# One decoder layer on one core: the pace at which modulation products are asked for during attention, 0.8 per unit throughout, becomes 1.5 in the first half and 0.6 in the second

## The chip, the core and the metric

The kernel runs on one core of a Trainium2 chip. Its engines work side by side, each in the order of its own instruction list: TensorE (PE; its weight loads are shown as PEld), VectorE (DVE), ScalarE (ACT), GpSimd (POOL) and SyncE (SP), which here does nothing but issue transfers, one after another. The metric is device time in microseconds for one execution, median of several runs; lower is better.

## The reference, cut to what matters

```python
mod = silu(c) @ w_ada + b_ada            # (1, 6 * 2048): six rows of 2048
sh1, sc1, gt1, sh2, sc2, gt2 = split(mod, 6)
h = rms_norm(x, g_pre_mix) * (1 + sc1) + sh1
proj = h @ w_in                          # q, k, v of 3 branches, gates, RG-LRU x and y
o_att = nsa_attention(...)               # 16 heads, 4 key groups, 512 queries
o_rnn = gelu(yr) * rg_lru(conv(xr))
x = x + gt1 * rms_norm(concat(norms of o_att, o_rnn) @ w_out, g_post_mix)
h = rms_norm(x, g_pre_mlp) * (1 + sc2) + sh2
x = x + gt2 * rms_norm(square(relu(h @ w_ff1)) @ w_ff2, g_post_mlp)
```

SEQ is 512, D_MODEL 2048, D_FF 8192, all in float32. The six rows of `mod` need 6 x 2048 dot products of length 2048 with `silu(c)`. Rows 0 and 1 are needed first, row 2 (`gt1`) in the output projection, rows 3 and 4 (`sh2`, `sc2`) at its end, row 5 (`gt2`) at the very end.

## The kernel before

The dot products for rows 2 to 5 are done on VectorE. One **product** (`qdot`, L219) loads a piece of `w_ada` (128 x 512, 256 KB, tile `md`) and multiplies it with a quarter of `silu(c)` that is copied to all partitions (tile `ca`), with the sum over its 512 columns as a by-product. A row has 64 products: 4 quarters by 16 pieces. The tile `ca` has one buffer, so the next quarter is loaded (L217) only when the 16th product of the one before has been done. The tiles `md` form a ring of 4 (`NMD`) during attention and share a ring of 6 (`NTMP`) in the output projection. Both loads are issued by SP, in the same list as the loads of the other weights (`wr`, L85: 512 KB each from `win`, `wv` or `wout`), which have a ring of their own of 2. A tool of the language sets the order of the instructions of each engine: it may put an instruction that is ready ahead of others that the code asks for earlier.

The stages that matter here, in order:

1. The first half of attention, `attention(0, n1)`: 64 units (a head, a branch, 128 queries). A unit takes scores (L727, L728 on TensorE), a softmax (`soft1` L737 and `soft2` L747 to L749 on VectorE and ScalarE), transposes (L756), the split of the transposed probabilities into two parts (`evac_t` L767, L768), and every fourth unit the product with the values (`pv` L783). `cmp_a` to `cmp_b` (L686 to L717) do the compressed branch. In between, TensorE works on the rest of the input projection (`proj`, L178 to L180), whose weights are split into a high and a low part (`sl`, L103 on ScalarE and L104 on VectorE), and the recurrent group runs (L804 to L850).
2. A transition: the keys, queries and values of the second pair of groups (L241, L254, L303).
3. The second half, `attention(1, n3 - n2)`, again 64 units.
4. The output projection: 4 column blocks of 512, 16 steps of k each, 4 x 3 matmuls of 512 columns per step (L916 to L918), results times `gbc` (L1073), with the remaining products of rows 3 and 4 spread over 36 steps (`cdots`), then residual and transposes.
5. The MLP, in which the products of row 5 are done at places of their own.

During attention, each of the 70 steps of a half adds `MRATE` to a counter, and a product is asked for each time it reaches 1. All products of row 2 come first, then row 4, then row 3. What is left of rows 4 and 3 is divided evenly over the steps of the output projection: `nd_ = [0.0, (len(QD[3]) + len(QD[4])) / 36.0]`.

Of the kernel before, what the change touches and what calls it, by code (L numbers as in the profile page):

```python
# [27 lines left out]
Q_REST, K_REST, XR_T, YR_T = 0, 6, 8, 16  # L28


NA1, NA2, NMS, NTMP, NXI, NPC, NSB, TD, MRATE, NMD, NRT = 4, 10, 22, 6, 4, 2, 11, 3, 0.8, 4, 6
JOIN = [2, 1, 1, 1] * 5 + [2, 1, 1, 0, 3]
KQ = 6
HALF, CA_ = 512, 1
# [97 lines left out]
def hybrid_block_kernel(ctx: ExitStack, tc: tile.TileContext, xT, c, vec, wada, wst, win, wv0, wv1,  # L132
# [125 lines left out]
    def fill(n):  # L258
        for _ in range(n):
            if stream:  # L260
                stream.pop(0)()
# [411 lines left out]
    def quad(pair, ep):  # L673
        return [((2 * pair + i % 2), 2 * ep + i // 2) for i in range(4)]
# [3 lines left out]
    def cmp_a(pair, ep):  # L678
        hs = quad(pair, ep)
        p_ = bp.tile([128, 4, 4, 32], F32, name="pc", tag="pc", bufs=1)  # L680
        for c2 in range(2):
            sc = ps("pj").rearrange("p (c e r n) -> p c e r n", c=2, e=4, r=2)
            for c_ in range(2):
                ch = 2 * c2 + c_
                for i, (g, e_) in enumerate(hs):
                    T.matmul(sc[:, c_, i].rearrange("p r n -> p (r n)"), Q[4 * g + e_][:, 128 * ch:128 * ch + 128],  # L686
                             kc[:, g].rearrange("p r n -> p (r n)"), start=True, stop=True)
            pv_ = p_[:, 2 * c2:2 * c2 + 2]
            V.tensor_add(pv_, sc[:, :, :, 0], maskc[:, 2 * c2:2 * c2 + 2, None, :].to_broadcast([128, 2, 4, 32]))
            V.tensor_add(pv_, pv_, sc[:, :, :, 1])  # L690
        m_ = bp.tile([128, 16], F32, name="cmx", bufs=1)
        d_ = bp.tile([128, 16], F32, name="cdn", bufs=1)
        pf = p_.rearrange("p c e n -> p (c e) n")
        V.reduce_max(m_, pf, axis=AX.X)
        V.tensor_sub(pf, pf, m_[:, :, None].to_broadcast([128, 16, 32]))
        A.activation(p_, p_, AF.Exp, scale=0.125)
        PC[pair, ep] = [p_, d_]

    def cmp_a2(pair, ep):
        p_, d_ = PC[pair, ep]  # L700
        pf = p_.rearrange("p c e n -> p (c e) n")
        V.reduce_sum(d_, pf, axis=AX.X)
        V.reciprocal(d_, d_)
        for i, (g, e_) in enumerate(quad(pair, ep)):
            dv = d_.rearrange("p (c e) -> p c e", c=4)[:, :, i]
            V.tensor_mul(dv, dv, gates[:, :, 3 * (4 * g + e_)])
        V.tensor_mul(pf, pf, d_[:, :, None].to_broadcast([128, 16, 32]))

    def cmp_b(pair, ep):
        p_, d_ = PC[pair, ep]  # L710
        pt = ps("pj")
        for ch in range(4):
            T.transpose(pt[:, 128 * ch:128 * ch + 128], p_[:, ch].rearrange("p e n -> p (e n)"), ident)
        ph = bp.tile([128, S], F32R, name="pch", bufs=1)
        pl = bp.tile([128, S], F32R, name="pcl", bufs=1)
        A.activation(ph, pt, AF.Copy)
        V.tensor_sub(pl, pt, f(ph))  # L717
        PC[pair, ep] = (ph, pl)
# [3 lines left out]
    def scores(u):  # L722
        h, br, ch = u
        n = 128 * (ch + 1)
        sp_ = ps("S")
        q_ = Q[h][:, 128 * ch:128 * ch + 128]
        T.matmul(sp_[:, :n], q_, KD[h // 4][:, br, 0, :n], start=True, stop=False)  # L727
        T.matmul(sp_[:, :n], q_, KD[h // 4][:, br, 1, :n], start=False, stop=True)  # L728
        UN[u] = [sp_]

    def soft1(u):
        h, br, ch = u
        n = 128 * (ch + 1)
        sp_ = UN[u][0]
        p_ = bp.tile([128, S], F32, name="pp", tag="pp", bufs=TD + 1)
        sm = bp.tile([128, 4], F32, name="sm", tag="sm", bufs=6)
        V.tensor_tensor_reduce(p_[:, :n], sp_[:, :n], mask[:, S - n:], scale=-0.125, scalar=3e38,  # L737
                               op0=OP.add, op1=OP.min, accum_out=sm[:, 0:1])
        A.activation(p_[:, :n], p_[:, :n], AF.Exp, bias=sm[:, 0:1], scale=-1.0, accum_out=sm[:, 1:2])
        UN[u] = [p_, sm]  # L740

    def soft2(u):
        h, br, ch = u
        n = 128 * (ch + 1)
        p_, sm = UN[u]
        gi = h * 3 + 1 + br
        V.reciprocal(sm[:, 2:3], sm[:, 1:2])  # L747
        V.tensor_mul(sm[:, 3:4], sm[:, 2:3], gates[:, ch, gi:gi + 1])
        A.activation(p_[:, :n], p_[:, :n], AF.Copy, scale=sm[:, 3:4])  # L749

    def trans(u):
        h, br, ch = u
        p_ = UN[u][0]
        pt = ps("T")
        for j in range(ch + 1):
            T.transpose(pt[:, 128 * j:128 * j + 128], p_[:, 128 * j:128 * j + 128], ident)  # L756
        UN[u] = [pt]

    def evac_t(u):
        h, br, ch = u  # L760
        n = 128 * (ch + 1)
        if ch == 0:
            HB[h, br] = [bp.tile([128, 13, 128], F32R, name=n_, bufs=1) for n_ in ("pth", "ptl")]
        th, tl = HB[h, br]
        pv_ = UN.pop(u)[0][:, :n].rearrange("p (j q) -> p j q", q=128)
        sl = slice(ch, 3 * ch + ch + 1, 3)
        A.activation(th[:, sl], pv_, AF.Copy)  # L767
        V.tensor_sub(tl[:, sl], pv_, f(th[:, sl]))  # L768
# [3 lines left out]
    def pv(h, br, i, pc):  # L772
        g = h // 4
        if br == 0:
            OT["o"] = ps("O")
            T.matmul(OT["o"], vcz[:, i], pc[0], start=True, stop=False)
            T.matmul(OT["o"], vcz[:, i], pc[1], start=False, stop=False)
        o = OT["o"]
        for j in range(4):
            v_ = VV[g][:, j, br].rearrange("p r d -> p (r d)")  # L780
            for x_, t_ in enumerate(HB[h, br]):
                m_ = t_[:, 4 * j:3 * j + 4].rearrange("p a b -> p (a b)")
                T.matmul(o[:, 128 * j:], v_, m_, start=False, stop=br == 1 and j == 3 and x_ == 1)  # L783

    def head_out(h, i, t):
        half = i % 2
        if half == 0:
            OT["t"] = bp.tile([128, S], F32, name="ot", bufs=1)
        ot, o = OT["t"], OT["o"]
        ol = rt("ol")  # L790
        A.activation(ol[0:64], o[64:128], AF.Copy)
        V.tensor_add(ot[64 * half:64 * half + 64], o[0:64], ol[0:64])
        if half:
            G.dma_start(oat[t], ot)
            add_sq(0, ot, t == 0)
# [150 lines left out]
    nmod = [0.0]  # L946

    def attention(pair, natoms):
        seq, info = [], {}
        for ep in range(2):  # L950
            for i, (g, e_) in enumerate(quad(pair, ep)):
                for br in range(2):
                    for ch in range(4):
                        u = (4 * g + e_, br, ch)
                        info[u] = (ep, i, 4 * pair + e_)
                        seq.append(u)
        n = len(seq)
        goal, done = len(stream) - natoms, 0
        for s_ in range(-1, n + TD + 2):
            def get(k):  # L960
                return seq[k] if 0 <= k < n else None
            if get(s_ - 1):
                soft2(get(s_ - 1))
            if get(s_ - TD - 1):
                evac_t(get(s_ - TD - 1))
            if get(s_):
                soft1(get(s_))
            if 0 <= s_ < n and s_ % 32 == CA_:
                cmp_a(pair, s_ // 32)
            if get(s_ + 1):  # L970
                scores(get(s_ + 1))
            tot = natoms * (s_ + 2) // (n + TD + 3)
            k = tot - done
            fill(k // 2)
            if get(s_ - TD):
                trans(get(s_ - TD))
            fill(k - k // 2)
            done = tot
            if 0 <= s_ < n:
                if s_ % 32 == CA_ + 1:  # L980
                    cmp_a2(pair, s_ // 32)
                if s_ % 32 == CA_ + 2:
                    cmp_b(pair, s_ // 32)
            u = get(s_ - TD - 1)
            if u and u[2] == 3:
                ep, i, t = info[u]
                pv(u[0], u[1], i, PC[pair, ep])
                if u[1] == 1:
                    head_out(u[0], i, t)
            nmod[0] += MRATE  # L990
            while nmod[0] >= 1:
                qdot(bp, 2 if QD[2] else 4 if QD[4] else 3, 1)
                nmod[0] -= 1
        fill(natoms - done)

    vcz_fill(0)
    attention(0, n1)
    evac_k(OT["k0"], 0, 1)
    evac_k(OT["k1"], 1, 1)
# [766 lines left out]
```

## Time and profile before

| what | value |
|---|---|
| median of 3 runs | 2195.1 us (2194.03 to 2197.76) |
| the profiled execution's own time | 2198.01 us |
| its span, first to last instruction | 2196.3 us |
| mean granted TensorE clock | 0.98 of full speed |
| TensorE, VectorE, ScalarE busy | 95%, 86%, 63% of the span |

The profile comes from one execution; durations are read from it. It began at 2196.3 us of span and took 1.7 us more around it, and was 2.9 us above the median of the runs.

### The profile page before, as it was taken

What the parts mean: (1) busy time and instruction counts of PE and PEld (TensorE: products, weight loads), DVE (VectorE), ACT (ScalarE), POOL (GpSimd) and SP (SyncE); (2) the same over time, 40 slices, a digit from 0 to 9 for tenths busy, and PEclk for the clock granted to TensorE, in tenths of its full rate; (3) what the DMA queues carried; (4) which work ended last, traced back from release to release, by engine and by line L of the source; (5) the groups of instructions that cost most, each with busy time, mean ns of one, the idle gap of its engine ahead of it and who ended that gap; (6) DMA issues with size and microseconds to landing.
All of it is one profiled execution on the core that took longest, in us unless ns stands there. A gap on an engine that the chain in (4) does not pass through costs nothing.

```text
span 2196.3 us, 39416 instructions
## 1 busy us (share of the span) xinstructions
PE 2095.3 (95%) x14621; PEld 1915.0 (87%) x14621; DVE 1878.7 (86%) x3764; ACT 1392.9 (63%) x2536; POOL 65.4 (3%) x121
## 2 busy tenths in 40 slices
PE   7998999999999989899999999998999999999995
PEld 3687777778877867899999999998999999999995
DVE  8987999877887677889999999998998878887788
ACT  4349879548995226765555555555866777767764
POOL 0000000000000000000000000000000000000010
PEclk8999999999999989999999999999999999999998
DMA  9764554662126886555555555566775444444453
GB/s 375 304 240 136 191 159 151 212 208 68 59 79 216 281 295 207 173 190 176 183 184 169 174 176 189 187 229 213 276 234 185 172 157 140 169 147 159 138 170 116
DMA packets 136802, 411.12 MB, mean 187 GB/s; under 512 B 16209, under 2 KB 23265, under 8 KB 132257
## 3 DMA queue, kind: packets, MB, share of 16 engines
q1 hardware_dynamic: 123970, 340.43, 45.9%
q0 software_dynamic: 12640, 68.17, 9.0%
q8 instruction: 115, 1.88, 0.3%
q14 instruction: 77, 0.63, 0.1%
HBM read 366.58 MB, written 41.97 MB: 186 GB/s over the span
## 4 chain that ended last, share of the span: by engine, by line
PE 64%; DVE 16%; DMA 8%; ACT 7%; issue 4%; SPq 0%; DVEq 0%; POOL 0%; ACTq 0%; POOLq 0%
PE ps_pj L1133 3%; DMA md<-wada 3%; PE ps_pj L1134 3%; PE ps_pj L1135 3%; PE ps_pj L1480 3%; PE ps_pj L1481 3%; PE ps_pj L1482 3%; DVE fl L1301 3%; PE ps_T L1135 2%; PE ps_T L1133 2%; PE ps_T L1134 2%; PE ps_S L1133 2%; PE ps_S L1134 2%; PE ps_S L1135 2%; PE ps_S L1480 2%
## 5 line engine op out<-in xcount | busy, mean ns | idle before, releaser
L1300 ACT ACTIVATE fh<-fs 128x1024 fp32r<-128x1024 f32 x256 | 272.9, 1066 | 326.8 <-DVE fs L1319 126.4
L1301 DVE TENSOR_TENSOR fl<-fs,fh 128x1024 fp32r<-128x1024 f32 x256 | 312.4, 1220 | 100.8 <-ACT fh L1300 98.2
L1300 ACT ACTIVATE fh<-fr 128x768 fp32r<-128x768 f32 (+2 forms) x296 | 217.2, 735 | 74.5 <-PE ps_pj L1134 12.9
L1301 DVE TENSOR_TENSOR fl<-fr,fh 128x768 fp32r<-128x768 f32 (+2 forms) x296 | 240.2, 814 | 14.4 <-ACT fh L1300 14.2
L103 ACT ACTIVATE sl<-wr 128x512 fp32r<-128x512 f32 (+2 forms) x252 | 145.5, 606 | 150.0 <-DMA wr<-wout 98.2
L104 DVE TENSOR_TENSOR sl<-wr,sl 128x512 fp32r<-128x512 f32 (+2 forms) x252 | 163.5, 662 | 46.9 <-ACT sl L103 32.2
L1316 DVE TENSOR_TENSOR fs<-fr 128x512 f32<-128x512 f32 x256 | 175.2, 684 | 8.2 <-DMA fr<-wff 6.6
L1480 PE MATMUL ps_pj<-fh,AH 128*128 128x256 f32 x602 | 168.9, 281 | 0.3 <-ACT ps_pj L1460 0.2
L1481 PE MATMUL ps_pj<-fl,AH 128*128 128x256 f32 x602 | 168.8, 281 | 0.0
L1482 PE MATMUL ps_pj<-fh,AL 128*128 128x256 f32 x602 | 168.2, 280 | 0.0
L178 PE MATMUL ps_pj<-AH,sl 128*128 128x512 f32 x384 | 162.4, 423 | 0.1
L219 DVE SCALAR_TENSOR_TENSOR md<-md,ca 128x512 f32<-128x512 f32 x192 | 127.3, 685 | 40.8 <-DMA md<-wada 23.3
L180 PE MATMUL ps_pj<-AH,sl 128*128 128x512 f32 x384 | 153.7, 400 | 2.0 <-DVE sl L104 1.9
L179 PE MATMUL ps_pj<-AL,sl 128*128 128x512 f32 x384 | 153.7, 400 | 0.0
L1480 PEld LDWEIGHTS ps_pj<-fh,AH 128*128 128x128 f32 x602 | 113.9, 189 | 0.9 <-ACT ps_pj L1460 0.9
L1481 PEld LDWEIGHTS ps_pj<-fl,AH 128*128 128x128 f32 x602 | 114.0, 189 | 0.2 <-DVE fl L1301 0.2
L1482 PEld LDWEIGHTS ps_pj<-fh,AL 128*128 128x128 f32 x602 | 113.6, 189 | 0.0
L1481 PE MATMUL ps_S<-fl,AH 128*128 128x256 f32 x394 | 110.8, 281 | 2.6 <-DVE fl L1301 2.6
L1480 PE MATMUL ps_S<-fh,AH 128*128 128x256 f32 x394 | 110.8, 281 | 2.0 <-ACT fh L1300 1.6
L1481 PE MATMUL ps_T<-fl,AH 128*128 128x256 f32 x396 | 110.9, 280 | 0.2 <-DVE fl L1301 0.2
L1480 PE MATMUL ps_T<-fh,AH 128*128 128x256 f32 x396 | 110.9, 280 | 0.0
L1482 PE MATMUL ps_T<-fh,AL 128*128 128x256 f32 x396 | 110.8, 280 | 0.0
(637 smaller groups left out, 7332.4 us busy)
## 6 DMA issues: line engine op xcount, KB each, us to landing
fr<-wff SPq DMA_DIRECT2D x276, 512.0 KB, 3.8
md<-wada SPq DMA_DIRECT2D x256, 256.0 KB, 4.5
uf<-ud POOLq DMA_DIRECT2D x32, 896.0 KB, 4.9
wr<-win SPq DMA_DIRECT2D x48, 512.0 KB, 3.7
ada<-wada SPq DMA_DIRECT2D x22, 1024.0 KB, 10.6
wr<-wout SPq DMA_DIRECT2D x36, 512.0 KB, 4.7
ud<-uf POOLq DMA_DIRECT2D x18, 896.0 KB, 5.3
ud<-uf POOLq DMA_DIRECT2D x14, 768.0 KB, 4.9
```

The source lines that it names most:

```text
L104: self.nc.vector.tensor_sub(lo, raw, self.f(hi))
L178: T.matmul(o, wh, mh, start=start, stop=False)
L179: T.matmul(o, wh, ml, start=False, stop=False)
L1133: T.matmul(o, wh, b[0], start=start, stop=False, skip_group_check=True)
L1134: T.matmul(o, wh, b[1], start=False, stop=False, skip_group_check=True)
L1135: T.matmul(o, wl, b[0], start=False, stop=stop, skip_group_check=True)
L1300: A.activation(hi, src, AF.Copy)
L1301: V.tensor_sub(lo, src, f(hi))
L1316: V.tensor_add(v2(Sm[:, :512]), v2(R[:, 256:768]), R[:, None, :256].to_broadcast([128, 2, 256]))
L1480: T.matmul(o, uh, hi, start=first and k < 4 and t_ == 0, stop=False, skip_group_check=True)
L1481: T.matmul(o, uh, lo, start=False, stop=False, skip_group_check=True)
L1482: T.matmul(o, ul, hi, start=False, stop=last, skip_group_check=True)
```

## The change

The rate becomes a pair, one number for each half of attention.

```diff
-NA1, NA2, NMS, NTMP, NXI, NPC, NSB, TD, MRATE, NMD, NRT = 4, 10, 22, 6, 4, 2, 11, 3, 0.8, 4, 6
+NA1, NA2, NMS, NTMP, NXI, NPC, NSB, TD, MR, NMD, NRT = 4, 10, 22, 6, 4, 2, 11, 3, (1.5, 0.6), 4, 6
...
-            nmod[0] += MRATE
+            nmod[0] += MR[pair]
             while nmod[0] >= 1:
                 qdot(bp, 2 if QD[2] else 4 if QD[4] else 3, 1)
                 nmod[0] -= 1
```

Where the products of rows 2, 3 and 4 then stand in VectorE's list:

| stage | before | of the change |
|---|---|---|
| first half of attention, up to its 64th `soft1` | 72 | 96 |
| transition, up to the 65th `soft1` | 40 | 40 |
| second half of attention | 0 | 10 |
| output projection | 80 | 46 |

VectorE in the first half, from the third to the next first chunk of queries of a branch (39th to 41st unit; `sm` and `pp` are the softmax, `ptl` the low part of the transposed probabilities, `sl` the low part of a split weight). Before:

```order
L737 ISA pp,sm<-ps_S,mask 128x384
L737 ISA sm 128x1
L748 TENSOR_TENSOR sm<-sm,gates 128x1
L737 ISA pp,sm<-ps_S,mask 128x512
L737 ISA sm 128x1
L768 TENSOR_TENSOR ptl<-ps_T,pth 128x3x128
L104 TENSOR_TENSOR sl<-wr,sl 128x512
L747 RECIPROCAL sm<-sm 128x1
L737 ISA pp,sm<-ps_S,mask 128x128
```

Of the change, the same units:

```order
L737 ISA pp,sm<-ps_S,mask 128x384
L737 ISA sm 128x1
L219 SCALAR_TENSOR_TENSOR md,dq_91<-md,ca 128x512 x2
L747 RECIPROCAL sm<-sm 128x1
L768 TENSOR_TENSOR ptl<-ps_T,pth 128x4x128
L748 TENSOR_TENSOR sm<-sm,gates 128x1
L737 ISA pp,sm<-ps_S,mask 128x512
L737 ISA sm 128x1
L104 TENSOR_TENSOR sl<-wr,sl 128x512
L219 SCALAR_TENSOR_TENSOR md,dq_91<-md,ca 128x512
L737 ISA pp,sm<-ps_S,mask 128x128
```

Where there were none, three products stand now between two softmaxes and the next; the splits and softmaxes keep their places.

VectorE at the end of the transition, from the last queries (`qd`, L254) to the second `soft1` of the second half. Before:

```order
L254 TENSOR_TENSOR qd<-ps_pj,qd 64x512 x2
L104 TENSOR_TENSOR sl<-wr,sl 128x512 x2
L737 ISA pp,sm<-ps_S,mask 128x128
L737 ISA sm 128x1
L747 RECIPROCAL sm<-sm 128x1
L748 TENSOR_TENSOR sm<-sm,gates 128x1
L737 ISA pp,sm<-ps_S,mask 128x256
```

Of the change:

```order
L254 TENSOR_TENSOR qd<-ps_pj,qd 64x512
L219 SCALAR_TENSOR_TENSOR md,dq_92<-md,ca 128x512
L254 TENSOR_TENSOR qd<-ps_pj,qd 64x512
L104 TENSOR_TENSOR sl<-wr,sl 128x512
L219 SCALAR_TENSOR_TENSOR md,dq_92<-md,ca 128x512 x3
L104 TENSOR_TENSOR sl<-wr,sl 128x512
L737 ISA pp,sm<-ps_S,mask 128x128
L737 ISA sm 128x1
L219 SCALAR_TENSOR_TENSOR md,dq_92<-md,ca 128x512
L747 RECIPROCAL sm<-sm 128x1
L748 TENSOR_TENSOR sm<-sm,gates 128x1
L737 ISA pp,sm<-ps_S,mask 128x256
```

Four products now stand between the first of the queries and the first softmax, and one behind that; from the first L254 to the reduction L694, which follows the third softmax, there are nine, where there was none.

SP in the output projection, in its third column block (`wr` are its weights). Before:

```order
L218 DMA md<-wada 128x512 x11
L85 DMA wr<-wout 128x1024
L218 DMA md<-wada 128x512 x5
L85 DMA wr<-wout 128x1024
L217 DMA ca<-cad 128x512
L218 DMA md<-wada 128x512 x3
L85 DMA wr<-wout 128x1024
L218 DMA md<-wada 128x512 x6
L85 DMA wr<-wout 128x1024
L218 DMA md<-wada 128x512 x4
```

Of the change:

```order
L85 DMA wr<-wout 128x1024 x5
L218 DMA md<-wada 128x512 x14
L217 DMA ca<-cad 128x512
L85 DMA wr<-wout 128x1024
L218 DMA md<-wada 128x512 x3
L85 DMA wr<-wout 128x1024
L218 DMA md<-wada 128x512 x3
L85 DMA wr<-wout 128x1024 x5
```

Before, groups of products stand between any two loads of weights; now five loads of weights stand together ahead of 14 products and five more behind a few.

## Rows read from the trace of the kernel before

**Rows 1.** The profile's page, part 1: busy us, share, instructions of each engine.

```profile
PE 2095.3 (95%) x14621; PEld 1915.0 (87%) x14621; DVE 1878.7 (86%) x3764; ACT 1392.9 (63%) x2536; POOL 65.4 (3%) x121
```

**Rows 2.** Five stretches: length, busy PE, PEld, DVE, ACT, POOL (instructions); clock, DMA, GB/s.

```profile
216.90:417.30 200.40, 192.11 (x980) 155.16 (x979) 188.03 (x616) 166.27 (x394) 3.95 (x7) 1.00 0.55 174
417.30:482.60 65.30, 60.40 (x372) 52.77 (x370) 47.98 (x127) 26.26 (x53) 0.54 (x1) 1.00 0.72 237
482.60:655.00 172.40, 166.09 (x847) 134.82 (x847) 142.63 (x447) 154.79 (x366) 3.25 (x6) 0.98 0.21 69
680.00:806.50 126.50, 126.50 (x546) 101.48 (x544) 89.48 (x209) 39.07 (x77) 0.00 (x0) 1.00 0.83 282
806.50:825.80 19.30, 10.37 (x25) 6.16 (x24) 13.62 (x32) 6.91 (x16) 0.00 (x0) 0.65 0.85 284
```

**Rows 3.** The same view for tile md alone; a product counts two instructions.

```profile
216.90:417.30 200.40, 48.93 (x144) 1.00 0.55 174
417.30:482.60 65.30, 26.71 (x80) 1.00 0.72 237
680.00:806.50 126.50, 41.92 (x128) 1.00 0.83 282
```

**Rows 4.** Waits of VectorE in the first half: us, times, longest.

```profile
DVE md L219 <- DMA ca<-cad: 3.8, 2, 2.3
DVE md L219 <- DMA md<-wada: 3.4, 4, 1.2
```

**Rows 5.** Timeline of VectorE: two products in a row (start, length).

```profile
747.96 0.69 DVE L219 SCALAR_TENSOR_TENSOR md<-md,ca 128x512 f32<-128x512 f32 x1
748.57 0.08 DVE L219 DVE_READ_ACCUMULATOR md<-md,ca 128x1 f32 x1
748.57 0.68 DVE L219 SCALAR_TENSOR_TENSOR md<-md,ca 128x512 f32<-128x512 f32 x1
```

**Rows 6.** Chain that ended last, first half: reloads of ca.

```profile
302.41 5.67 DMA ca<-cad
...
399.91 4.37 DMA ca<-cad
```

**Rows 7.** Timeline of VectorE around the second half's first units.

```profile
480.52 0.69 DVE L254 TENSOR_TENSOR qd<-ps_pj,qd 64x512 fp32r<-64x512 f32 x1 [0.66 <-ACT qd L253]
...
483.45 0.16 DVE L747 RECIPROCAL sm<-sm 128x1 f32<-128x1 f32 x1 [0.56 <-ACT pp L739]
...
484.83 0.17 DVE L747 RECIPROCAL sm<-sm 128x1 f32<-128x1 f32 x1 [0.68 <-ACT pp L739]
```

**Rows 8.** Timeline of TensorE in the same place.

```profile
481.36 1.12 PE L686 MATMUL ps_pj<-kc,qd 128*128 128x64 f32 x8 [2.27 <-DVE qd L254]
...
494.26 0.63 PE L713 MATMUL ps_pj<-vecs,pc 128*128 128x128 f32 x4 [0.64 <-DVE pc L707]
```

**Rows 9.** All engines in two pieces of that place: granted clock behind POOL.

```profile
484.00:486.00 2.00, 2.00 (x6) 1.54 (x6) 1.31 (x6) 1.27 (x4) 0.00 (x0) 0.50 0.41 168
...
490.00:492.00 2.00, 2.00 (x13) 1.64 (x12) 1.94 (x6) 1.98 (x5) 0.00 (x0) 1.00 0.00 0
```

**Rows 10.** Timeline of TensorE in the third column block of the output projection.

```profile
806.43 0.39 PE L918 MATMUL ps_pj<-sl,AL 128*128 128x512 f32 x1
812.11 0.79 PE L916 MATMUL ps_pj<-sl,AH 128*128 128x512 f32 x1 [5.29 <-ACT sl L103]
...
817.66 0.79 PE L917 MATMUL ps_pj<-sl,AH 128*128 128x512 f32 x1 [3.18 <-DVE sl L104]
```

**Rows 11.** Timeline of SP in the same block (L85 loads output weights).

```profile
766.45 8.97 SPq L218 DMA_DIRECT2D md<-wada  x11
775.51 0.38 SPq L85 DMA_DIRECT2D wr<-wout  x1
...
804.70 0.38 SPq L85 DMA_DIRECT2D wr<-wout  x1
```

## The prediction, as put on record before the changed kernel was run

> **What bounds the kernel now.** I read the page first: TensorE is busy 95% of the span, VectorE 86% [rows 1]. Such shares are an average over stages, and the change touches three of them, so I cut the trace into stretches [rows 2].
>
> The first half of attention (216.9 to 417.3, 200.4 us) has VectorE busy 188.0 us. It is idle 12.4 us, and 7.2 us of that are waits of products for their own transfers: 3.8 us for the next quarter of silu(c), 3.4 us for pieces of w_ada [rows 4]. So only 5 us of 200 are left in which VectorE waits for another engine. This stage goes at VectorE's pace. TensorE shows 192.1 us there, which looks as full. But it loads weights 155.2 us of 200.4, 77%, against 101.5 of 126.5, 80%, in the output projection, where it never pauses [rows 2]; and since many of attention's matmuls have fewer columns, so that a weight load is a larger part of each, a TensorE without pauses would show more than 80% here. It has at least 7 us of room (3 in 80 of 200).
>
> The Trainium skill (Perfetto Trace Analysis, Identifying the Most-Contended Engine) says that matmul busy time tells little of how full TensorE is, and that the share of weight loading tells more. By matmul time, TensorE would set the pace here and up to 8 us more VectorE work could hide; by weight loading VectorE sets it. I follow the second reading, which the 5 us above bear out without it.
>
> The transition (65.3 us) has 40 products and VectorE busy 48.0 us; TensorE is busy 60.4 us and sets the pace. The second half has no product at all [rows 3]; VectorE is busy 142.6 of 172.4 us.
>
> In the output projection from 680 to 806.5, TensorE does not pause: 546 matmuls in 126.5 us, 0.232 us each. Then it starves: 5.29 us and 3.18 us of waiting for split weights [rows 10], at a granted clock that falls to the lower level (1.2 GHz) on the way, 0.65 in the mean over 806.5 to 825.8 [rows 2]. In these 19.3 us it does 25 matmuls, 5.8 us' worth: 13.5 us are lost. The reason stands in SP's list: loads of output weights wait behind loads for products, which wait for buffers of the ring (11 of them take 8.97 us to issue) [rows 11], and the transfers carry 282 GB/s already [rows 2].
>
> **The change part by part.** A product takes 0.69 us, but the next instruction starts 0.61 us after it [rows 5]; 0.61 us is its price where VectorE sets the pace.
>
> First half, +24 products: 14.6 us. By the order shown, two splits of weights move behind the 64th unit and one split of probabilities ahead of it, together about -1 us. That is +13.6 us of VectorE work in a stage where it has nothing to hide behind, since I count only the 5 us of other waits as cover. Next the reloads of the quarter: a reload starts when the 16th product is done and takes 4.4 to 5.7 us [rows 6]. Before, there were four behind the first one; two were covered by other work and two cost 3.8 us together [rows 4]. Now there are five, at the 17th, 33rd, 49th, 65th and 81st product, and in the new order only one to three splits and some softmax instructions stand between the 16th product and the 17th. Bounds: all covered, which gives back 3.8 us; or each costs the longest of before, 2.3 us, 11.5 in all, +7.7. I take +4, nearer the upper end, as the cover has become regular and short. From the waits for other engines, and because TensorE now runs further ahead of VectorE at the end of the stage, I take off 2. Sum for the stage: **+15.5 us**, between +6 (all 7.2 us of transfer waits gone) and +21 (13.6 + 7.7).
>
> Transition: 40 products as before, and TensorE sets the pace. **0**, with 3 us either way.
>
> Second half, +10 products, and in the transition four that move from ahead of the last queries to behind them. Nine of them stand between the first L254 and the reduction L694, that is in the chain on which TensorE waits: 2.27 us for L254 and 0.64 us for L707 [rows 8]. Nine by 0.61 us are 5.5 us. The waits of VectorE there, 0.66, 0.56 and 0.68 us [rows 7], take 1.9 of it: +3.6 us. TensorE runs at the lower clock in this place (0.50 at 484, 1.00 again at 490) [rows 9], and a longer pause keeps it there a little longer: +0.4. The other five stand in units where VectorE has 17% of its time free [rows 2]: 0, at worst their 3 us and a reload. Sum **+4 us**, 0 to +9.
>
> Output projection, -34 products, that is 34 x 256 KB less to load. A step of k needs 256 KB of output weights in 12 x 0.232 = 2.8 us. Before, 80 products over 36 steps added 569 KB to it, 300 GB/s together, a little more than the 282 that the transfers carried [rows 2]. With 46 it is 327 KB, 210 GB/s. The starving has no reason left; the worst remnant is the burst of 14 loads for products in SP's list, but five loads of weights stand ahead of it. Gain: **-13 us** of the 13.5; at the other bound a second pause of 5.29 us remains, with its part of the lower clock, and the gain is -6.
>
> Sum: 15.5 + 0 + 4 - 13 = **+6.5 us**. The profiled execution (2198.0 us) would become 2204.5; it lies 2.9 us above the median of the runs, so the median goes from 2195.1 to about **2202 us**, 0.3% slower. A measurement of this kernel tells a change from none at about 0.2%, 4.4 us.
>
> **The rivals.**
>
> *Faster: the first half hides the products.* One mechanism: TensorE sets the pace of the first half, as its 192.1 of 200.4 busy us suggest, and the 12.4 idle us of VectorE take up the 13.6. Then the stage grows by 2 us, and the sum is 2 + 4 - 13 = -7: **2188 us**. It decides when both halves together grow by less than 8.6 us. Against it: VectorE's idle time is mostly waits for its own transfers, and more products bring more of those. Chance 0.13.
>
> *About the same: the waits for transfers vanish.* The new order spaces the products evenly, so that every transfer lands in time and the 7.2 us of waits go; first half +6.4, second +4, output -13: -2.6, **2192.5 us**, with the neighbours from -4.4 to +2. For it: the evenness. Against it: the short cover of the reloads. Chance 0.17.
>
> *Slower still: the output projection goes on starving.* What holds the loads of weights back is then not the products but the ring of two, which is free only when VectorE has split a piece. Gain -6 instead of -13: +13.5, **2208.5 us**. Against it: 126 us without a pause, and a pause that comes where transfers are fullest. Chance 0.12.
>
> *Slower still: the clock.* If the reloads make TensorE pause in the first half as it did ahead of L686 at 481, its clock can fall there as it did then [rows 8, 9]: some 6 us at half speed, 3 us, for each of three or four reloads: +10 on top, **2212 us**. The Trainium skill (TensorE: Matmul & The Clock Gate, Why this matters for your kernels) warns of idle gaps between bursts of matmuls; the row of the first half shows a clock of 1.00 throughout [rows 2], so the pauses of before did not bring it on. Chance 0.08.
>
> That the products would not move at all is excluded: the new order shows where each stands.
>
> **How the numbers follow.** The forecast, +1 to +13, has 0.50. Of it 0.13 lies under +4.4 us and counts as the same. So faster 0.13; the same 0.17 + 0.13 = 0.30; slower 0.37 + 0.12 + 0.08 = 0.57. The range leaves out about a tenth at each end: from -5, where most of the faster case begins, to +16: 2190 to 2211.
>
> **What would show it.** In the changed profile: the first half, from its first to its 64th softmax, at 213 to 219 us instead of 200.4, with VectorE busy about 202 of it and TensorE's weight loading at about 72%; waits of VectorE for the quarter's reload near 8 us; the 65th softmax some 65 us behind the 64th; TensorE's wait before L713 grown to 2 us or more and the second half 4 us longer; the output projection's third block without a pause and at full clock from 680 on. It is wrong if the first half grows by less than 8 us (then VectorE did not set the pace, or the waits went), or if TensorE still pauses over 3 us in the third column block.

## The result, and the profile after

The changed kernel took 2208.3 us (median of 4 runs, 2205.89 to 2210.81), the kernel before beside it 2195.3 us: a ratio of 1.0054, with a 95% interval of 1.0039 to 1.0069. It is slower by half a per cent, 13.0 us. The prediction was 2202.0 us, in a range of 2190 to 2211, with "slower" as its likeliest sign.

The profiled execution took 2208.55 us with a span of 2206.8, 10.5 more than that of before. The page's part 1 of the changed kernel:

```profile
PE 2101.0 (95%) x14621; PEld 1917.9 (87%) x14621; DVE 1877.8 (85%) x3764; ACT 1393.2 (63%) x2536; POOL 65.2 (3%) x121
```

The whole-kernel shares are those of [rows 1], so nothing can be seen there. Here are the stages, in columns like [rows 2]: first half (from its first to its 64th softmax), transition, second half, output projection, and a piece of the output projection from its first to its third column block.

```profile
217.30:435.70 218.40, 202.35 (x984) 160.14 (x983) 201.03 (x654) 166.90 (x394) 3.95 (x7) 0.97 0.58 187
435.70:505.60 69.90, 59.85 (x365) 52.29 (x365) 50.65 (x140) 25.68 (x52) 0.54 (x1) 0.98 0.76 241
505.60:691.00 185.40, 176.74 (x884) 143.27 (x885) 154.81 (x482) 162.53 (x380) 3.78 (x7) 0.95 0.26 85
691.00:877.90 186.90, 185.52 (x816) 147.84 (x815) 123.45 (x262) 80.54 (x174) 0.54 (x1) 1.00 0.68 225
706.40:840.00 133.60, 133.60 (x576) 107.16 (x576) 87.50 (x187) 48.28 (x96) 0.00 (x0) 1.00 0.74 250
```

The kernel before, for the last two stages cut in the same way (the first two are in [rows 2]):

```profile
482.60:664.30 181.70, 175.32 (x884) 142.55 (x884) 149.45 (x462) 162.08 (x380) 3.79 (x7) 0.95 0.23 74
664.30:865.50 201.20, 190.93 (x813) 149.44 (x814) 145.31 (x334) 80.63 (x174) 0.54 (x1) 0.97 0.76 257
```

| stage | before | of the change | difference | predicted |
|---|---|---|---|---|
| first half | 200.4 | 218.4 | +18.0 | +15.5 |
| transition | 65.3 | 69.9 | +4.6 | 0 |
| second half | 181.7 | 185.4 | +3.7 | +4 |
| output projection | 201.2 | 186.9 | -14.3 | -13 |

These add up to +12.0. The stretch ahead of them is 0.4 longer, the one behind 1.9 shorter: +10.5. The profiled execution of before was 2.7 us above its median, that of the change 0.3 above, which makes the 13.0 of the medians.

The same view for tile md alone (the first three stages) has 96, 40 and 10 products, two instructions each, against 72, 40 and 0 in [rows 3]:

```profile
217.30:435.70 218.40, 64.44 (x192) 0.97 0.58 187
435.70:505.60 69.90, 26.85 (x80) 0.98 0.76 241
505.60:691.00 185.40, 6.93 (x20) 0.95 0.26 85
```

The waits of VectorE in the first half (total, times, longest), which answer to [rows 4]:

```profile
DVE sm L747 <- ACT pp L739: 8.5, 10, 1.5
DVE md L219 <- DMA ca<-cad: 5.3, 5, 1.6
...
DVE md L219 <- DMA md<-wada: 0.4, 1, 0.4
```

Reloads of the quarter cost 5.3 us instead of 3.8, pieces 0.4 instead of 3.4. Together the transfer waits are 1.5 us shorter than before. The largest wait is one that before came to only 1.0 us: the reciprocal of a softmax waits for ScalarE.

VectorE's waits in the transition, before:

```profile
DVE md L219 <- DMA md<-wada: 9.2, 10, 2.4
DVE md L219 <- issue: 3.6, 1, 3.6
DVE md L219 <- DMA ca<-cad: 3.4, 1, 3.4
```

The one under "issue" (nothing that the profile shows) is a wait for a reload as well. The timeline of SP and VectorE has that reload, and the next product, the 81st, which is the first to need it; the two reloads of this stage took 4.5 and 5.3 us to land:

```profile
427.60 0.33 SPq L217 DMA_DIRECT2D ca<-cad  x1
...
432.97 0.69 DVE L219 SCALAR_TENSOR_TENSOR md<-md,ca 128x512 f32<-128x512 f32 x1 [3.61 <-issue]
```

The waits of the change:

```profile
DVE md L219 <- DMA ca<-cad: 11.5, 3, 5.8
DVE md L219 <- DMA md<-wada: 6.5, 7, 2.0
```

So 40 products wait 18.0 us for transfers instead of 16.2: three reloads cost 11.5 us instead of two 7.0, one of them 5.8 alone, and pieces 6.5 instead of 9.2. VectorE also has 2.7 us more work in this stage (50.65 us against the 47.98 of [rows 2]), other instructions that the new order moved there. What stands behind a waiting product is late, as the waits of TensorE there show, the answer to L686 in [rows 8]:

```profile
PE ps_pj L686 <- DVE qd L254: 4.3, 1, 4.3
PE ps_T L756 <- DVE ptl L768: 2.5, 1, 2.5
```

Of TensorE's waits in the second half the first has grown (0.8 us before), one of 0.6 us is new (L178), and L713 is no longer among them:

```profile
PE ps_S L727 <- DVE sm L737: 4.4, 4, 2.1
```

In the output projection one pause is left, 1.2 us at its beginning, and the third block has none of those in [rows 10]; in the piece from 706.4 to 840 TensorE does 576 matmuls in 133.6 us, 0.232 each, at a clock of 1.00.

The clock did fall in the first half, at three places: from 287 to 291, from 342 to 346 and from 373 to 380. All engines in two pieces at the last of them, the clock behind POOL:

```profile
369.30:373.30 4.00, 0.82 (x3) 0.30 (x2) 4.00 (x7) 2.61 (x8) 0.00 (x0) 0.98 0.38 131
373.30:377.30 4.00, 3.53 (x9) 2.81 (x10) 4.00 (x15) 3.19 (x7) 0.54 (x1) 0.50 0.62 183
```

and the timeline of VectorE and of TensorE there:

```profile
367.69 0.69 DVE L219 SCALAR_TENSOR_TENSOR md<-md,ca 128x512 f32<-128x512 f32 x1 [1.03 <-DMA ca<-cad]
...
370.13 2.33 DVE L843 TENSOR_TENSOR_SCAN ti<-tr,ti 128x512 f32<-128x512 f32 x2
...
382.72 0.17 DVE L747 RECIPROCAL sm<-sm 128x1 f32<-128x1 f32 x1 [1.24 <-ACT pp L739]
```

```profile
370.96 0.50 PE L178 MATMUL ps_pj<-AH,sl 128*128 128x512 f32 x1 [1.57 <-ACT sl L103]
...
373.77 0.58 PE L727 MATMUL ps_S<-kd,qd 128*128 128x256 f32 x1 [2.08 <-DVE sm L737]
...
375.89 0.63 PE L180 MATMUL ps_pj<-AH,sl 128*128 128x512 f32 x1
376.31 0.63 PE L178 MATMUL ps_pj<-AH,sl 128*128 128x512 f32 x1
```

VectorE waits for a reload, does its products and then a scan. TensorE runs dry, pauses 1.57 and 2.08 us, and goes on with 0.42 us between two matmuls instead of 0.23, at the lower level (1.2 GHz). Then VectorE in its turn waits for a softmax.

### The profile page after: what moved, and what is told of

Read it like the earlier page. It is cut to its first block, busy times and chain, and to the rows that moved or that the text cites. A ratio compares the mean times of both kernels' runs of the same rounds, so it can differ in the third digit from the quotient of the medians.

```text
span 2206.8 us, 39393 instructions
## 1 busy us (share of the span) xinstructions
PE 2101.0 (95%) x14621; PEld 1917.9 (87%) x14621; DVE 1877.8 (85%) x3764; ACT 1393.2 (63%) x2536; POOL 65.2 (3%) x121
## 4 chain that ended last, share of the span: by engine, by line
PE 68%; DVE 14%; DMA 8%; ACT 7%; issue 3%; POOL 0%; DVEq 0%; SPq 0%; ACTq 0%; POOLq 0%
PE ps_pj L1133 3%; PE ps_pj L1134 3%; PE ps_pj L1135 3%; DMA md<-wada 3%; PE ps_pj L1481 3%; PE ps_pj L1480 3%; PE ps_pj L1482 3%; PE ps_T L1133 2%; PE ps_T L1135 2%; PE ps_T L1134 2%; PE ps_S L1133 2%; PE ps_S L1134 2%; PE ps_S L1135 2%; DVE md L219 2%; DVE fl L1301 2%
## 5 line engine op out<-in xcount | busy, mean ns | idle before, releaser
L1300 ACT ACTIVATE fh<-fr 128x768 fp32r<-128x768 f32 (+2 forms) x296 | 217.0, 735 | 69.3 <-PE ps_pj L1134 11.3
L178 PE MATMUL ps_pj<-AH,sl 128*128 128x512 f32 x384 | 161.3, 420 | 4.6 <-ACT sl L103 3.4
L1319 DVE TENSOR_TENSOR fs<-fs,fr 128x256 f32<-128x256 f32 x256 | 108.0, 422 | 3.7
## 6 DMA issues: line engine op xcount, KB each, us to landing
ada<-wada SPq DMA_DIRECT2D x22, 1024.0 KB, 10.2
```

What stands on the lines that cost most here:

```text
L178: T.matmul(o, wh, mh, start=start, stop=False)
L1300: A.activation(hi, src, AF.Copy)
```

## The experiments

The lengths below are those of the four stages in each kernel's own trace. Products are counted in VectorE's list, those of the second half up to its last softmax; in experiments 3 and 10 three and four more run behind that softmax before the output projection begins.

**1. The first half of the change alone** (96 / 15 / 0 / 81; 35 products of the change's transition and second half fall to the output projection).

```diff
-... TD, MR, NMD, NRT = ... 3, (1.5, 0.6), 4, 6
+... TD, MR, NMD, NRT = ... 3, (1.5, 0.1), 4, 6
```

> Rates 1.5 and 0.1: the products stand 96, 15, 0 and 81 (first half, transition, second half, output projection; before: 72, 40, 0, 80). The first half as in the change, the output projection as before. Theory (VectorE paces the first half, each product there costs 0.61 us and its reloads some more): first half about 218 us as in the change (before 200.4), transition 62 to 66 us, TensorE's pause in the output projection stays; +13 to +18 us against before. Rival (the growth comes from the whole of attention's transfers, not from the first half's products): with 25 products fewer in the transition the first half stays below 210 us and the sum below +8 us.

Measured: 2202.07 us, ratio 1.0038 (1.0024 to 1.0052). First half and transition:

```profile
217.80:436.20 218.40, 201.26 (x983) 159.14 (x982) 201.07 (x654) 166.94 (x394) 3.96 (x7) 0.97 0.58 187
436.20:491.30 55.10, 54.15 (x339) 48.06 (x339) 34.59 (x86) 26.19 (x52) 0.54 (x1) 1.00 0.54 173
```

The 18 us of the first half are its own. But the transition, with 15 products instead of 40, takes 10.2 us less than before, and not the 62 to 66 us that were expected, so that the sum is +9.4 us against before and not 13 to 18: with 40 products in it, TensorE does not set its length.

**2. The rest of the change alone** (72 / 44 / 31 / 45).

```diff
-... (1.5, 0.6), 4, 6
+... (0.8, 1.3), 4, 6
```

> Rates 0.8 and 1.3: the products stand 72, 44, 31 and 45. The output projection as in the change, the first half as before, 31 products in the second half instead. Theory: first half about 200 us as before; 31 x 0.61 = 19 us of VectorE work in the second half, which has 30 us free of 172, costs 3 to 8 us; output projection without a pause, -13 to -14; -4 to -9 us against before. Rival (the second half is as tight as the first, each product costs its 0.61 us): +15 to +19 there, 0 to +6 us against before.

Measured: 2189.32 us, ratio 0.9974 (0.9959 to 0.9988), faster than both kernels. Second half and output projection:

```profile
483.20:668.70 185.50, 175.62 (x885) 141.32 (x885) 165.12 (x528) 162.61 (x380) 3.80 (x7) 0.96 0.36 116
668.70:855.50 186.80, 185.46 (x816) 147.88 (x815) 123.00 (x260) 80.41 (x174) 0.54 (x1) 1.00 0.68 224
```

In the second half 31 products cost 3.8 us; in the first half 24 more cost 18.0. The output projection gives its 14.4 us back wherever the products have gone.

**3. The rates of before, with each product of attention kept at its place in the code** (53 / 4 / 48 / 87).

```diff
-            (V.scalar_tensor_tensor(w, w, 0.5, CA[0], ...
+            i_ = V.scalar_tensor_tensor(w, w, 0.5, CA[0], ...
+            if ring[0] == "md":
+                tc.keep_in_program_order(i_)
```

> Rates 0.8 and 0.8 as before, but every product of attention is kept behind the VectorE instruction that precedes it in the code, so that it is not put ahead: 53, 4, 48 and 87. Theory: the first half loses 19 x 0.61 = 11.6 us of VectorE work and gets 7 to 12 us shorter (188 to 193 us), down to what TensorE needs; the transition 0 to 4 us shorter; the second half, with 48 x 0.61 = 29 us in 30 free, 4 to 12 us longer; the output projection with 7 products more 1 to 5 us longer; -8 to +6 us in all. Rival (VectorE does not pace the first half; its waits for transfers do): first half 197 us or more, +5 to +15 us in all.

Measured: 2199.31 us, ratio 1.0028 (1.0013 to 1.0043). First and second half:

```profile
217.40:414.40 197.00, 189.77 (x973) 154.27 (x973) 178.90 (x574) 165.77 (x394) 3.96 (x7) 1.00 0.48 151
470.30:668.00 197.70, 180.46 (x914) 144.19 (x912) 174.91 (x568) 162.29 (x381) 3.79 (x7) 0.96 0.43 138
```

With 19 products less the first half is only 3.4 us shorter, and VectorE is idle for 18 us of it. The rival's figures came out (197.0 us, +6.6 in all), but not its reason: VectorE's waits for transfers are 4.2 of those 18 us. I took the result as TensorE's own floor of 197 us, which experiment 8 refutes. That a fixed place in the list costs something itself fits both halves (48 products cost the second 16.0 us, where experiment 10 has 61 for 9.5), but is not shown apart.

**4. The change, with products that multiply 256 of their 512 columns** (101 / 45 / 0 / 46; half of each sum is left out, the loads are whole).

```diff
-            (V.scalar_tensor_tensor(w, w, 0.5, CA[0], ...
+            (V.scalar_tensor_tensor(w[:, :256], w[:, :256], 0.5, CA[0][:, :256], ...
```

> The change, but each product of rows 2 to 4 multiplies and sums only 256 of its 512 columns, while all of its 256 KB is loaded: the other half of the sum is left out, and the transfers stay. The order puts 101, 45, 0 and 46 products. Theory (VectorE's work sets the pace of the first half): a product costs about 0.34 us instead of 0.61, 27 us less for a hundred of them, and the first half falls from 218 us to 188 to 198, where TensorE's own work ends it; -8 to -20 us against before. Rival (the transfers of the products, or SP's list, pace the first half): it stays above 212 us, +5 to +12 us against before.

Measured: 2192.10 us, ratio 0.9997 (0.9984 to 1.001). First half and transition:

```profile
216.00:423.10 207.10, 191.31 (x972) 154.05 (x972) 182.25 (x672) 166.35 (x394) 3.96 (x7) 1.00 0.63 206
423.10:493.00 69.90, 62.30 (x376) 54.02 (x374) 41.29 (x142) 25.92 (x52) 0.54 (x1) 0.96 0.76 247
```

The first half gives back 11.3 us, between what the theory and its rival said: VectorE has less work there than before the change (182.3 us against 188.0), but waits 13.0 us for transfers instead of 7.2. The transition stays at 69.9 us with 9 us less work for VectorE: it now waits 28.3 us for transfers instead of 18.0.

**5. The change, with loads of half the bytes** (96 / 43 / 7 / 46; 256 columns are loaded and used twice).

```diff
...
+            if ring[0] == "md":
+                nc.sync.dma_start(w, wada[s_, k, :, S * q_:S * q_ + S // 2])
+                h2 = lambda a: a.rearrange("p (a b) -> p a b", a=2)
+                V.scalar_tensor_tensor(h2(j_), w[:, None, :].to_broadcast([128, 2, 256]), 0.5, h2(CA[0]), ...
```

> The changed kernel, but a product asked for in attention loads only 256 of its 512 columns and uses them twice, so that VectorE does the same work with half the bytes; half of each of these sums is left out. Products stand 96 / 43 / 7 / 46. Theory (VectorE sets the pace of the first half, transfers that of the transition): the first half stays at 214 to 219 us with VectorE busy about 201, and the transition falls from 69.9 us to 55 to 62; total 2194 to 2203. Rival (the bytes of the products pace the first half, as the half-width run allows): the first half falls to 200 to 208 us. Second rival (the transition's length comes from VectorE's work or from TensorE): it stays at 68 to 70.

Measured: 2193.50 us, ratio 0.9994 (0.9982 to 1.0005).

```profile
216.30:428.50 212.20, 196.46 (x974) 157.28 (x973) 200.17 (x655) 166.29 (x392) 3.94 (x7) 0.98 0.42 132
428.50:490.60 62.10, 59.52 (x372) 52.97 (x370) 52.96 (x145) 26.49 (x53) 0.54 (x1) 1.00 0.63 195
```

The transition falls by 7.8 us, as the theory said. The first half falls by 6.2, more than it said, and less than if the bytes set its pace.

**6. The change, without reloads of silu(c)** (96 / 44 / 6 / 46).

```diff
-            if k == 0 or CA["pool"] is not pool:
+            if CA.get("pool") is not pool:
```

> The changed kernel, but silu(c) is copied to all partitions once in a stage, its first quarter, and not again for the next quarters; products of the other quarters use the wrong quarter, so that part of the sums is left out. Theory: VectorE's waits for the reload (5.3 us in the first half, 11.5 us in the transition) are real costs: first half 212 to 215 us instead of 218.4, transition 59 to 65 instead of 69.9, output projection unchanged at 186 to 188 since VectorE's waits there are off the path; total 2194 to 2202. Rival (the reloads only hide other waits: for ScalarE's softmax in the first half, for the pieces' own transfers in the transition): first half 217 to 219, transition 68 to 70, total 2205 to 2211.

Measured: 2192.97 us, ratio 0.9992 (0.9983 to 1.0001).

```profile
215.60:427.30 211.70, 197.45 (x976) 157.50 (x976) 200.61 (x654) 166.16 (x393) 3.95 (x7) 0.98 0.58 187
427.30:493.50 66.20, 60.59 (x372) 53.81 (x370) 52.93 (x149) 26.22 (x53) 0.54 (x1) 0.98 0.78 258
```

The first half falls by 6.7 us for 5.3 us of waits: the reloads are a real cost there. The transition falls by 3.7 for 11.5: the waits for pieces grow by 4.9 (11.4 us now), and it has four products more, 2.3 us of work.

**7. The change without any load for attention's products** (96 / 49 / 1 / 46; all use one piece and one quarter, their sums are left out).

```diff
+                if CA.get("wp") is not pool:
+                    ...
+                    nc.sync.dma_start(CA["w"], wada[s_, k, :, S * q_:S * q_ + S])
+                    ...
+                V.scalar_tensor_tensor(j_, CA["w"], 0.5, CA[0], op0=OP.mult, op1=OP.mult, ...
```

> The changed kernel, but the products asked for in attention load nothing: all use one piece of w_ada and one quarter of silu(c), loaded once in the stage, so that their sums are left out and VectorE's work alone is there; products stand 96 / 49 / 1 / 46. Theory (VectorE paces the first half once work is added, by its 201 us of work and some 6 to 8 us of waits for ScalarE's softmax): first half 205 to 210 us; transition 55 to 60 us although it has 49 products, because its length comes from their transfers. Rival for the first half (the transfers of pieces and quarters made all of the 18 us): 198 to 202. Rival for the transition (VectorE's work paces it): 68 or more.

Measured: 2180.36 us, ratio 0.9936 (0.9919 to 0.9953).

```profile
216.40:423.30 206.90, 196.41 (x975) 157.97 (x975) 200.01 (x655) 165.76 (x393) 3.95 (x7) 0.98 0.22 68
423.30:480.40 57.10, 57.10 (x355) 50.83 (x354) 55.76 (x157) 26.80 (x53) 0.54 (x1) 1.00 0.32 103
```

Both stages come out as the theory said. The first half is left with VectorE's work and 6.9 us in which it waits for other engines. In the transition TensorE does not pause at all, with 49 products beside it.

**8. The kernel before with the same edit** (73 / 39 / 0 / 80).

> The kernel before with the same edit: products 73 / 39 / 0 / 80, none of attention's loading anything. Theory (TensorE sets a floor of about 197 us for the first half, and the kernel before lies 3 us above it by its transfers): first half 196 to 198 us, transition 55 to 57; the 23 products that the run beside it has more in the first half then cost 9 to 13 us there as VectorE work alone, and the rest of the change's 18 us is transfers. Rival (VectorE sets the pace of the first half before, too, and its waits for transfers are real): 192 to 195 us, 7 us less than before. Second rival (its transfer waits are covered): 199 to 201.

Measured: 2180.80 us, ratio 0.9933 (0.9916 to 0.9951).

```profile
216.80:409.90 193.10, 188.54 (x972) 154.56 (x972) 188.86 (x617) 165.86 (x393) 3.95 (x7) 1.00 0.23 75
409.90:466.40 56.50, 56.22 (x349) 49.80 (x348) 48.33 (x126) 26.73 (x53) 0.54 (x1) 1.00 0.29 98
```

My theory of that moment (TensorE's floor of 197 us) falls, and the rival is right: without its loads the first half takes 193.1 us, of which VectorE works 188.9. The 7.3 us that it gains match the 7.2 us of waits in [rows 4]. The run beside it has 23 products more in the first half and takes 13.8 us longer, 0.60 us for each.

**9. Rates of 0.8 and 1.0** (72 / 44 / 10 / 66).

```diff
-... (1.5, 0.6), 4, 6
+... (0.8, 1.0), 4, 6
```

> Rates 0.8 and 1.0: products stand 72 / 44 / 10 / 66; the second half as in the change, the first as before, and the output projection between the two. Theory: first half 199 to 201 us, transition 67 to 70, second half 184 to 186 (ten products cost what 31 cost, because the cost lies in the few at its start), and the output projection 187 to 190, since 66 products ask for 256 + 469 KB in 2.8 us, 259 GB/s, still under the 282 that were carried. Rival for the output projection (each product costs the same there, 0.42 us): 194 to 196. Rival for the second half (a product costs 0.12 us wherever it stands): 182.5 to 183.5.

Measured: 2194.35 us, ratio 0.9997 (0.9987 to 1.0007).

```profile
486.00:669.90 183.90, 175.79 (x884) 142.75 (x885) 154.72 (x483) 162.33 (x380) 3.78 (x7) 0.96 0.27 85
669.90:862.00 192.10, 188.35 (x816) 148.59 (x815) 136.52 (x306) 79.79 (x174) 0.54 (x1) 0.99 0.76 250
```

The second half falls between theory and rival: inconclusive. So does the output projection: from 46 to 66 products it grows by 5.2 us (0.26 each), from 66 to the 80 of before by 9.1 (0.65 each). It bends where the arithmetic of bytes expected it, but softly.

**10. Rates of 1.0 and 1.0, the transition kept free of products** (70 / 3 / 61 / 58): the first four products of the second half stay behind what the code has ahead of them.

```diff
-... (1.5, 0.6), 4, 6
+... (1.0, 1.0), 4, 6
...
+            if CA.get("pin", 0) > 0:
+                CA["pin"] -= 1
+                tc.keep_in_program_order(i_)
...
+    CA["pin"] = NMD
     attention(1, n3 - n2)
```

> Rates 1.0 and 1.0, and the first four products of the second half kept behind the code that is ahead of them, so that none can be drawn into the transition: 70 / 3 / 61 / 58 instead of 96 / 40 / 10 / 46. Theory (a product costs nothing where VectorE still waits for others, and some 0.4 to 0.6 us in a full stage or in the transition): first half 198 to 201 us, transition 55 to 56, second half 188 to 194 with VectorE busy about 187, output projection 187 to 191; median 2178 to 2188, faster than the kernel before. Rival (61 products are too many for the second half, as 48 made it 197.7 us when each was kept in program order): second half 199 to 206, median 2190 to 2198.

Measured: 2179.71 us, ratio 0.9934 (0.992 to 0.9948), the fastest kernel here that computes everything. Its four stages:

```profile
216.50:415.30 198.80, 190.40 (x978) 154.79 (x978) 187.25 (x611) 164.93 (x393) 3.95 (x7) 1.00 0.55 174
415.30:471.80 56.50, 55.79 (x345) 48.99 (x344) 25.81 (x52) 27.12 (x54) 0.54 (x1) 1.00 0.32 100
471.80:663.00 191.20, 177.67 (x907) 141.85 (x905) 181.87 (x594) 163.67 (x382) 3.78 (x7) 0.97 0.51 161
663.00:852.60 189.60, 188.62 (x821) 150.09 (x821) 129.78 (x280) 82.00 (x175) 0.54 (x1) 0.99 0.71 235
```

All four lie within or next to what the theory expected. The second half takes 61 products (65 up to the output projection) for 9.5 us, 0.15 to 0.16 each; emptying the transition gives 8.8 us, the lighter output projection 11.6.

## Why the prediction was right, and where its terms were off

The sign and the main mechanism held: VectorE's work came into a stage that goes at VectorE's pace, and the relief of the output projection did not pay for it. The loss was twice the forecast (13.0 us against 6.5 in the sum), and the mechanism of one stage, the transition, was wrong.

**Who sets the pace of the first half.** The reading was right: VectorE, with TensorE having at least 7 us of room. Experiment 8 shows it directly, since TensorE did the same stage in 193.1 us instead of 200.4 once VectorE no longer waited for its loads. ScalarE's waits for loads of weights, which might have gained by that run too, were 1.1 us before and 1.6 us there. The section of the Trainium skill that the prediction leaned on (Perfetto Trace Analysis, Identifying the Most-Contended Engine) agrees with the traces in this: for the same matmuls of this stage TensorE shows 188.5 us of matmul time in experiment 8, 192.1 before and 202.4 in the change (the last at a mean clock of 0.97), so that time is not what TensorE needs. Its weight loading, 155.2 us before and 154.6 in experiment 8, hardly moved.

**First half, +15.5; measured +18.0.** The term for the work was sized well: 13.6 predicted, 13.0 more busy us measured (201.03 against 188.03). The two small terms were wrong, and that their errors partly cancelled was luck. Reload waits were to grow by 4: they grew by 1.5 (8 us expected in all, 5.3 found), and the waits for pieces fell by 3.0, so the waits for transfers came out 5.5 us under the forecast. The waits for other engines were to fall by 2: they grew by 6.5 (from 5.2 of 12.4 idle us to 11.7 of 17.4), 8.5 over the forecast, and the one for ScalarE's softmax alone grew by 7.5. So this is the mis-sized step, "From the waits for other engines ... I take off 2".

Half of the ten softmax waits can be followed back in the trace. Three of them (at 293.18, 379.38 and 382.72, 3.4 us together) stand behind matmuls at the lower clock. Two more (at 269.97 and 432.11, 2.5 us together) stand behind a wait of ScalarE itself for a load of weights:

```profile
267.52 0.63 ACT L103 ACTIVATE sl<-wr 128x512 fp32r<-128x512 f32 x1 [2.02 <-DMA wr<-win]
...
430.66 0.63 ACT L103 ACTIVATE sl<-wr 128x512 fp32r<-128x512 f32 x1 [2.09 <-DMA wr<-win]
```

ScalarE splits weights and does its part of the softmax in one list, and SP's list has the loads of weights among those of the products. ScalarE's waits for weights from `win` went from 1.1 us before to 7.5 in the change; with half the bytes (experiment 5) they are 4.6, without loads (experiment 7) 2.0. So the transfers cost more than VectorE's waits for them: the first half without loads is 7.3 us shorter at the rates of before (200.4 - 193.1) and 11.5 at those of the change (218.4 - 206.9), where VectorE's own waits for transfers are 7.2 and 5.7. By these runs the +18.0 are 13.8 of work (206.9 - 193.1) and 4.2 of loads. Without reloads alone the stage fell by 6.7 us, yet 7.6 us of softmax waits were left. The order of the list differs between all these kernels, and what it adds by itself is not settled.

**Transition, 0; measured +4.6.** This step failed, and the measured change lies outside its bound of 3 us: "TensorE sets the pace" there. It rested on TensorE's 60.4 busy us of 65.3. The reading that the prediction used for the first half would have said otherwise: VectorE's 48.0 us of work and its 16.2 us of waits for its own transfers make 64.2 of the 65.3 us. With 3 or 4 products the stage takes 56.5 or 55.9 us, with 15 it takes 55.1; with 40 to 44 whole ones 65.3 to 69.9; with 43 of half the bytes 62.1; with 49 that load nothing 57.1. Against the runs without loads, the transfers cost 8.8 us before (65.3 - 56.5) and 12.8 in the change (69.9 - 57.1): VectorE stands at a product's load, and what TensorE needs stands behind that in VectorE's list. (Some of that comes back later: in the shorter transition of experiment 8 TensorE does 349 matmuls instead of 372, and the second half is 1.4 us longer, so over both stages the loads of before cost 7.4 us.) The 4.6 us of the change are about 2.7 of more work in VectorE's list and 1.8 of longer waits for transfers. With three reloads instead of two and products ahead of the last queries, TensorE's wait for L254 went from 2.27 to 4.3 us.

**Second half, +4; measured +3.7.** Right in size, in part by luck: four of the nine products that it counted stand ahead of the stage's first softmax, so that their delay fell to the transition. The sign that was named for it, a longer wait before L713, did not come. The delay lies ahead of it instead: in the transition at L686, and in the second half at L727, whose wait for the softmax went from 0.8 to 4.4 us. That products further inside the stage cost little holds by experiments 2 and 10 (31 for 3.8 us, 61 to 65 for 9.5).

**Output projection, -13; measured -14.3.** Right, with its mechanism: no pause in the third block, full clock. The rival in which it goes on starving is out; its 2208.5 us lie next to the measured time by the errors above, and not by its cause.

**The clock.** The rival gave 0.08 to a fall in the first half at a price of 10 us. It fell, at three places for some 4 to 7 us each, to 0.97 in the mean over the stage. The warning of the Trainium skill that was cited for it (TensorE: Matmul & The Clock Gate, Why this matters for your kernels) is borne out by the row at 373.3, with 0.50. The rival's reason is not: only that place has a reload's wait ahead of it. Ahead of the other two TensorE pauses 1.82 and 1.09 us behind a scan (at 285 and 287) and 1.53 us for L707 (at 341), and without any loads (experiment 7) the clock fell twice as well. A single pause of 1.70 us before the change (at 406.57) brought no fall. Three softmax waits, 3.4 us, stand behind the falls; all waits for other engines grew by 6.5 us, so in VectorE's list the clock cost less than the 10 of the rival.

**Within the spread:** the 1.9 us that the kernel gains behind the output projection, where the change touches nothing. That stretch takes 1325.7 to 1330.8 us in the traces of these kernels.

## What to carry to other kernels

Ask of each stage in which engine's list the work waits, not only which engine is fullest: before the change TensorE was busy 92 to 97% of each of these four stages, and in two of them VectorE's list, held up by loads of its own, set the length. Add such an engine's waits for its own transfers to its busy time before deciding how much room is left (195 of 200.4 us in the first half, 64 of 65.3 in the transition), and look up what a wait under "issue" was for; a run in which that work loads nothing shows the rest. Work that can stand anywhere belongs where its engine waits for others anyway: here one product cost 0.75 us in the first half (18.0 for 24), 0.24 in the transition (8.8 for 37), 0.26 to 0.65 in the output projection, and 0.12 to 0.16 in the second half for 31 and 61 of them (the change's ten cost 0.37 each, 48 at fixed places 0.33). Emptying the transition and spreading the products over both halves (experiment 10) made the kernel 0.66% faster than before, instead of 0.54% slower.

## What the runs showed of the hardware

A reload that copies one row of 512 values to all 128 partitions took 3.8 to 4.9 us to land in the first half of the changed kernel, where transfers carry 187 GB/s, and 4.3 to 7.1 us in its transition at 241 GB/s; VectorE waited for it at most 1.6 us in the one and up to 5.8 us in the other. Pauses of TensorE of 1.57 and 2.08 us within 4 us (granted clock 0.98) were followed by 0.50 over the next 4 us; a pause of 2.27 us had gone ahead of the 0.50 of before [rows 8, 9].
